# Inverses of triangular blocks in a hybrid recurrent layer: TensorE doubling in place of VectorE steps

## The chip, the core and the metric

One core of a Trainium2 chip runs the whole kernel. The metric is device time in microseconds of one execution. The engines are TensorE (PE, with its weight loads shown as PEld), VectorE (DVE), ScalarE (ACT), GpSimd (POOL) and SyncE (SP, which issues the DMAs). They run beside each other and wait for one another by semaphores.

## What is computed

One layer of a decoder trunk over a prompt of 1024 tokens and 8 sample tokens, width 1024. A normed input is projected to the columns of four mixers (GLA, S5, a gated delta net, RWKV-7), each mixer runs its recurrence, its output is gated, and one output projection and a final norm follow. What matters here are the two mixers with a triangular system per block of 64 tokens. The delta net states it openly:

```python
low = jnp.where(strict, jnp.einsum('nbhid,nbhjd->nbhij', kb, k) * decay, 0.0)
tmat = low + jnp.eye(c, dtype=low.dtype)          # c = 64
sol = lax.linalg.triangular_solve(tmat, rhs, left_side=True, lower=True, unit_diagonal=True)
u, w = sol[..., :HEAD_DIM], sol[..., HEAD_DIM:]
def step(s, inp):                                 # over the blocks of a sequence
    uu, ww, qd, kd, at, gt = inp
    v_new = uu - jnp.einsum('bhcd,bhdv->bhcv', ww, s)
    o = jnp.einsum('bhcd,bhdv->bhcv', qd, s) + jnp.einsum('bhij,bhjv->bhiv', at, v_new)
    s = gt[..., None, None] * s + jnp.einsum('bhcd,bhcv->bhdv', kd, v_new)
    return s, o
```

RWKV-7 is given as a step per token; the kernel brings it to the same blocked form, again with the inverse of a unit lower triangular 64 x 64 matrix per block and head.

## The kernel before

The sequence is worked in two halves of 512 tokens (the second with the 8 sample tokens), and in each half a mixer is two units, one per pair of heads. A unit is a Python generator of stages: its projections, its preparation, for RWKV and the delta net its inverses (stage 2), and the recurrence over eight blocks (stage 3). The string ORDER names the units in the order in which their next stages are emitted (R, D, L for RWKV, delta net and GLA, S for S5, W for S5's weights, g for a gate, a tick for the second half; 97 tokens), and PRI gives a stage a head start in priority ("R2" is stage 2 of an R unit). From that a scheduler that simulates a timeline fixes the order of every engine's queue; on the chip each engine takes its queue strictly in that order.

A projection (`stream`, line 269) loads 128 columns of weights in two quarters by DMA, splits each into two parts (ACT at line 265, POOL at line 266) and runs 24 matmuls per piece of 260 or 512 tokens at line 277. These matmuls are more than half of TensorE's busy time, and the weight loads (line 262) are issued from SP's queue in their turn.

`inverse` (line 287) is called at the start of stage 2 (lines 446 and 656), eight times in all: two mixers, two pairs, two halves. One call inverts 16 matrices of 64 x 64. Each is cut into two 32 x 32 diagonal blocks, so there are 64 blocks, and one block below. Before the change:

- The blocks go from their tiles to DRAM (d1, line 297) and come back in LT with one block per partition, copied to four groups of 32 partitions (line 300); DT is loaded with rows of the unit matrix (dinit).
- 31 steps on VectorE, each a product (line 307, into DP) and a sum (line 309, into DT), build the inverses.
- DT goes to DRAM (d2, line 312) and into the diagonal blocks of XT (line 314).
- Line 318 transposes the first diagonal block on VectorE; the matmuls of lines 323 and 326, eight per parity of the block, each with an eviction by ACT (lines 324 and 327), form the block off the diagonal.

The recurrences (`mm` at lines 483 and 689) then use XT: in each of the eight steps matmuls alternate with VectorE (r, U or UV at line 122, r at line 693, the state at lines 499 and 702) and ACT copies the output (lines 500 and 703). Their PSUM tiles come from `psc`, a tag with four buffers, as do those of `inverse`.

The GLA unit has a loop of six levels whose products `lw0` and `lw1` are put on VectorE or POOL by the table ENG (line 116 executes them).

Of the kernel before, what the change touches and what calls it, by code (L numbers as in the profile page):

```python
# [16 lines left out]
T = 1024  # L17
# [7 lines left out]
NB = dict(ta=9, pr=11, on=3, gp=8, sh=2, kA=6, XT=2, Gt=5, s8=4, ss=4, wr=3, wh=2, wl=2, d1=1, LT=1, DT=2, DP=1, d2=2, Dn=2, w8=2, rf=1,  # L25
# [4 lines left out]
           glu="V", g5="V", cvm="V", l2="V", sgl1="V", sgl2="V", lw0="V", lw1="G", ld0="G", ld1="G", lqk="V", rS="A", rr="V",  # L30
# [18 lines left out]
for _b, _n, _w, _p in (("A", "ident", 128, 128), ("A", "vec", NVEC, 128), ("B", "bones", 128, 128), ("B", "maskG", 256, 128),  # L49
                       ("B", "onesr", 1, 128), ("B", "wlora", 256, 128), ("B", "i64", 64, 128),  # L50
                       ("B", "negD", 128, 128), ("B", "Jm", 128, 128),
                       ("B", "wg2", 256, 16), ("B", "st_shift", 7 * NS, 128), ("B", "st_conv", 18 * NS, 128)):
    CONST[_n] = (_b, CONST_W[_b], _p)
    CONST_W[_b] += _w
# [9 lines left out]
def trunk(ctx: ExitStack, tc: tile.TileContext, I, O):  # L64
# [20 lines left out]
    def cload(name, shape):  # L85
        """A block of columns of the constants that one transfer brings."""
# [7 lines left out]
    def late(ins, after):  # L94
        """Schedule ins, which nothing else holds back, only when after has been issued: its tile waits for its turn."""
# [18 lines left out]
    def tt(name, out, a, b, op=ALU.mult):  # L114
        """out = a op b on the engine that ENG names."""
# [14 lines left out]
    def load_x(h, after=None):  # L130
        """The rows of a half and the gains of its norm."""
# [11 lines left out]
    # ------------------------------------------------------------ constants  # L143
# [10 lines left out]
    i64 = cload("i64", (128, 64))  # L154
    onesr = cload("onesr", (128, 1)).to_broadcast([128, 128])
# [17 lines left out]
    # what is carried from the first half of the sequence to the second  # L173
# [22 lines left out]
    def sig_arg(e, x, bias=None):  # L196
        """e = x (+ bias), bounded where exp(-x) would run out of the range of Ln: 1 / (1 + e^43) < 2^-62."""
# [5 lines left out]
    def sig_chain(e, *outs):  # L203
        """sigmoid(e) to each (out, columns of e)."""
# [8 lines left out]
    def sample_bc(src):  # L213
        """[128 (h, v), 8] -> PSUM [128 (h, any), 8, 64]: each head's values along the free dim."""
# [6 lines left out]
    def mat_vec(S, col):  # L221
        """sum over keys i of S[(h, i), b, v] * col[(h, i), b], on all partitions of the head."""
# [46 lines left out]
    def stream(wsrc, evac):  # L269
        """evac(PSUM [128, m], c0, m) for the columns of (128 columns of w).T @ x."""  # L270
# [15 lines left out]
    # ------------------------------------------------------------ inverses of unit lower triangular matrices  # L286
    def inverse(Ga, XT, after):
        """XT[64 p + s, k, t] = ((I - L) ** -1)[t, s] for the 16 strictly lower L[t, s] = Ga[p][..][s, k, t] of a unit;
        p is the parity of a chunk and k = (pair of chunks, head), in one or two tiles."""
        Q = [(p, f) for p in range(2) for f in range(2)]  # L290
        at = lambda p, f: slice(64 * p + 32 * f, 64 * p + 32 * f + 32)
        d1 = drp.tile([2, 2, 8, 32, 32], F32, tag="d1", bufs=NB["d1"], name="d1")
        for p, f in Q:
            r = slice(32 * f, 32 * f + 32)
            nb = 8 // len(Ga[p])
            for b, g in enumerate(Ga[p]):
                SP.dma_start(out=d1[p, f, nb * b:nb * b + nb].rearrange("(c e) s t -> s c e t", e=2), in_=g[r, :, :, r])
        LT = tmp.tile([128, 32, 32], F32, tag="LT", bufs=NB["LT"], name="LT")
        for q in range(4):
            SP.dma_start(out=LT[32 * q:32 * q + 32], in_=d1.rearrange("p f x s t -> (p f x) s t"))  # L300
        DT = tmp.tile([128, 8, 32], F32, tag="DT", bufs=NB["DT"], name="DT")
        late(SP.dma_start(out=DT.rearrange("p m i -> p (m i)"), in_=I["dinit"]), after)
        for j in range(31):
            m = j // 4 + 1
            w = 31 - j
            tp = tmp.tile([128, 8, 32], F32, tag="DP", bufs=NB["DP"], name="DP")
            V.tensor_tensor(tp[:, :m, :w], DT[:, :m, j:j + 1].to_broadcast([128, m, w]),  # L307
                            LT[:, j:j + 1, j + 1:32].to_broadcast([128, m, w]), ALU.mult)
            V.tensor_tensor(DT[:, :m, j + 1:32], DT[:, :m, j + 1:32], tp[:, :m, :w], ALU.add)  # L309
# [1055 lines left out]
def lay_out(inp):  # L1365
    import numpy as np
    z = lambda *s: np.zeros(s, np.float32)
    a = {}
# [141 lines left out]
```

## Time and profile before

| | us |
|---|---|
| median of 3 runs | 1070.27 |
| lowest, highest | 1069.81, 1078.98 |
| profiled execution, first to last instruction (its span) | 1069.0 |

The profile gives no time of its own for the profiled execution beside its span. The lowest run is 0.8 us above the span, the median 1.3 us: that is what lies around it. Busy time of an engine is the union of its instructions' times; a TensorE record lasts until its results are out, so successive records overlap. The granted clock is the share of 2.4 GHz that TensorE got; 0.5 is the lower of its two levels, and a mean between 0.5 and 1 says how the time was divided.

### The profile page before, as it was taken

The numbers are of one execution on the slowest core, as the hardware profiler recorded it, in microseconds if no ns is written. First come the engines' busy times: TensorE is split into PE (matmuls) and PEld (weight loads), VectorE is DVE, ScalarE is ACT, GpSimd is POOL, SyncE is SP. The second block draws the span as 40 slices with busy tenths as digits, with TensorE's granted clock in tenths as the row PEclk, the third lists the DMA queues.
The fourth block names the chain that finished last, engine by engine and source line by source line (L and its number), as shares of the span: only waits on it lengthen the run. The fifth ranks groups of instructions, "written<-read, shape, count | busy, mean of one in ns | idle before, by whom it ended". The sixth has DMA issues, their size and how long they took to land. (4 is left out here: it accounts for less than half of the span.)

```text
span 1069.0 us, 16993 instructions
## 1 busy us (share of the span) xinstructions
PE 928.3 (87%) x5994; PEld 762.7 (71%) x5994; DVE 704.2 (66%) x1871; ACT 459.6 (43%) x1033; POOL 395.3 (37%) x434
## 2 busy tenths in 40 slices
PE   3899889979999788897989898988989989769794
PEld 3676657658777576797788767677868958658694
DVE  8528884668648864736578989979875366553514
ACT  4355544332644343522753454643235235162634
POOL 2788654531321441133363403125326312313231
PEclk9999979876898666798999889888888569869898
DMA  7133414210211132224223223311112014612532
GB/s 235 50 127 106 115 59 111 71 54 21 74 49 43 46 93 81 81 79 148 69 85 97 77 76 83 92 47 50 53 59 71 22 66 126 212 49 79 183 128 86
DMA packets 76804, 92.23 MB, mean 86 GB/s; under 512 B 41400, under 2 KB 43584, under 8 KB 76720
## 3 DMA queue, kind: packets, MB, share of 16 engines
q1 hardware_dynamic: 76720, 91.16, 27.2%
q8 instruction: 47, 0.77, 0.3%
q14 instruction: 37, 0.30, 0.1%
HBM read 74.38 MB, written 14.62 MB: 83 GB/s over the span
## 5 line engine op out<-in xcount | busy, mean ns | idle before, releaser
L266 POOL TENSOR_TENSOR wl<-wr,wh 128x512 fp32r<-128x512 f32 x152 | 204.6, 1348 | 420.5 <-ACT wh L265 403.6
L277 PE MATMUL psp<-xhi,wh 128*128 128x260 f32 (+2 forms) x728 | 262.2, 361 | 10.7 <-DVE rx L355 6.5
L277 PE MATMUL psp<-xhi,wl 128*128 128x260 f32 (+2 forms) x728 | 256.3, 355 | 5.2 <-POOL wl L266 5.0
L277 PE MATMUL psp<-xlo,wh 128*128 128x260 f32 (+2 forms) x728 | 253.3, 349 | 0.8 <-DVE xlo L257 0.8
L277 PEld LDWEIGHTS psp<-xhi,wh 128*128 128x128 f32 x728 | 153.2, 210 | 33.8 <-issue 12.8
L277 PEld LDWEIGHTS psp<-xhi,wl 128*128 128x128 f32 x728 | 151.2, 209 | 25.4 <-POOL wl L266 7.4
L265 ACT CAST wh<-wr 128x512 fp32r<-128x512 f32 x152 | 93.7, 618 | 172.3 <-PE psp L277 92.9
L277 PEld LDWEIGHTS psp<-xlo,wh 128*128 128x128 f32 x728 | 153.2, 211 | 16.7 <-issue 3.8
L307 DVE TENSOR_TENSOR DP<-DT,LT 128x60 f32<-128x60 f32 (+24 forms) x248 | 81.9, 330 | 12.5 <-DMA XT<-d 3.1
L309 DVE TENSOR_TENSOR DT<-DT,DP 128x60 f32<-128x60 f32 (+24 forms) x248 | 73.8, 297 | 6.1
L277 PE MATMUL psp<-ohi,wh 128*128 128x260 f32 (+1 forms) x192 | 65.5, 342 | 5.4 <-ACT yT L1295 3.5
L277 PE MATMUL psp<-olo,wh 128*128 128x260 f32 (+1 forms) x192 | 64.0, 334 | 1.8 <-DVE olo L116 1.8
L277 PE MATMUL psp<-ohi,wl 128*128 128x260 f32 (+1 forms) x192 | 62.9, 334 | 0.0
L1303 DVE TENSOR_TENSOR xf<-psb,xf 128x128 f32<-128x128 f32 x64 | 14.5, 282 | 49.6 <-PE psb L1301 41.3
L277 PEld LDWEIGHTS psp<-ohi,wh 128*128 128x128 f32 x192 | 37.7, 197 | 8.5 <-ACT yT L1295 3.9
L762 PE MATMUL psb<-W 64*128 64x64 f32 x256 | 40.7, 331 | 1.8 <-DVE DT L309 1.8
L112 ACT ACTIVATE eg<-eg 128x260 f32<-128x260 f32 (+1 forms) x72 | 34.0, 486 | 18.2 <-DVE eg L199 17.4
L277 PEld LDWEIGHTS psp<-olo,wh 128*128 128x128 f32 x192 | 37.7, 196 | 4.6 <-DVE olo L116 2.1
L762 PEld LDWEIGHTS psb<-W 64*128 64x128 f32 x256 | 36.4, 237 | 5.7 <-issue 3.1
L277 PEld LDWEIGHTS psp<-ohi,wl 128*128 128x128 f32 x192 | 37.0, 195 | 2.4 <-POOL wl L266 0.2
L116 POOL TENSOR_TENSOR df<-cum 128x256 f32<-128x256 f32 x48 | 30.8, 663 | 17.2 <-DVE cum L737 15.2
L483 PE MATMUL psc<-UV,Gt 64*128 64x64 f32 (+1 forms) x256 | 35.6, 288 | 0.6 <-ACT UV L476 0.6
(423 smaller groups left out, 1862.4 us busy)
## 6 DMA issues: line engine op xcount, KB each, us to landing
wr<-in_wct SPq DMA_DIRECT2D x120, 256.0 KB
wr<-in_wo SPq DMA_DIRECT2D x32, 256.0 KB
xn<-in_x SPq DMA_DIRECT2D x8, 512.0 KB
LT<-d SPq DMA_DIRECT2D x32, 128.0 KB
xf<-in_x SPq DMA_DIRECT2D x8, 512.0 KB
out_y<-xf SPq DMA_DIRECT2D x8, 512.0 KB
dgp<-gp SPq DMA_DIRECT2D x8, 256.0 KB
Gml<-dG SPq DMA_DIRECT2D x4, 512.0 KB
```

What stands on the lines that cost most here:

```text
L112: A.activation(out, in_, func, bias=bias, scale=scale, **kw)
L116: return (G if ENG[name] == "G" else V).tensor_tensor(out, a, b, op)
L265: A.copy(hi, raw)
L266: G.tensor_tensor(lo, raw, hi, ALU.subtract)
L277: X["mm"] = PE.matmul(p[:, :m], w[:, k % 4, :], x[:, k, c0:c0 + m], start=(k == 0 and s == 0), stop=(k == 7 and s == 2))
L307: V.tensor_tensor(tp[:, :m, :w], DT[:, :m, j:j + 1].to_broadcast([128, m, w]), LT[:, j:j + 1, j + 1:32].to_broadcast([128, m, w]), ALU.mult)
L309: V.tensor_tensor(DT[:, :m, j + 1:32], DT[:, :m, j + 1:32], tp[:, :m, :w], ALU.add)
L483: PE.matmul(o, l, r, start=start, stop=True, skip_group_check=True)
L762: PE.matmul(pg[:, c, :], W[HS[e], t], W[HS[e], t].rearrange("p (b f s) -> p f b s", f=2, s=s)[:, 1], start=True, stop=True)
L1303: V.tensor_tensor(xf[j][:, cols], pt[:, j, :], xf[j][:, cols], ALU.add)
```

## The change

`inverse` builds the 32 x 32 inverses on TensorE by doubling the size of the blocks that are already inverted: 1, 2, 4, 8, 16 to 32. The running inverse is kept in the PSUM tile `acc`. At each of five levels 32 matmuls (four quadrants, eight matrices each) multiply the blocks with the inverse so far (Xn), VectorE evicts the product through a mask that leaves the blocks of this level (LX), 32 more matmuls add the correction to acc, and VectorE transposes acc (Xn) while ACT copies it (Xt) for the next level. The four quadrants lie on the diagonal of the array: rows and columns 32 q to 32 q + 31. The off-diagonal block is formed as before, with both parities in one loop. The DMA round trips, LT, DT, DP and dinit go; two masks of constants, `imask` and `i32`, join the blob constB. The product lw1 goes from POOL to VectorE, five priorities are lowered (R2, D3, L1, R1, L2), and ORDER is rearranged.

```diff
-NB = dict(... d1=1, LT=1, DT=2, DP=1, d2=2, Dn=2, ...
+NB = dict(... LX=2, Xn=2, Xt=2, ...
-ENG = dict(... lw1="G", ...
+ENG = dict(... lw1="V", ...
-PRI = {"R2": 4000, "D2": 1000, "R3": 4000, "D3": 4000, "L1": 2000, "R1": 600, "L0": 100, "L2": 600, "D0": 300, "D1": 1000}
-ORDER = ("x W t W m W R0 g6 R0 D0 W W M W D0 D1 R1 W R0 R1 R0 L0 R1 R1 L0 D1 L0 g0 D0 D0 S g0 L1 g4 g6 g3 g7 L1 D1 g2 D1 g5 "
-         "L1 x' g7 g1 g4 S t' R1' R1' m' R0' g1 R1' g3 M' R1' R0' g2 D0' g5 R0' D1' D0' L1' g1' g7' R0' D0' D1' g4' g6' D0' "
-         "L0' L1' L1' D1' g2' g7' g0' L0' D1' g6' g4' L0' S' g5' g3' S' g3' g0' g2' g5' g1' T T'")
+PRI = {"R2": 620, "D2": 1000, "R3": 4000, "D3": 2000, "L1": 900, "R1": 380, "L0": 100, "L2": 300, "D0": 300, "D1": 1000}
+ORDER = ("x W t W m W g6 R0 D0 R0 W W M W D0 W D1 R1 R1 R0 L0 R1 R1 R0 L0 D1 L0 g0 D0 g0 L1 g4 g6 g3 L1 D1 D0 S g2 g7 D1 g5 L1 "
+         "x' g7 g1 g4 S t' R1' R1' R0' m' g1 R1' g3 R1' R0' D0' L1' M' g2 D0' g5 R0' D1' g1' g7' R0' D0' D1' D0' g4' g6' L0' L1' "
+         "D1' g2' g7' g0' L1' L0' g4' D1' g6' L0' S' g5' g3' g1' S' g3' g0' g2' g5' T T'")
+    imask = cload("imask", (128, 160))
+    i32 = cload("i32", (128, 32))
     def inverse(Ga, XT, after):
         Q = [(p, f) for p in range(2) for f in range(2)]
         at = lambda p, f: slice(64 * p + 32 * f, 64 * p + 32 * f + 32)
...
+        nb = 8 // len(Ga[0])
+        gat = lambda p, f, k, t: Ga[p][k // nb][32 * f:32 * f + 32, k % nb // 2, k % 2, t]
+        one = i32.rearrange("p (o t) -> p o t", o=1).to_broadcast([128, 8, 32])
+        acc = psc(128, 8, 32)
+        def mm(o, l, r, start, first=None):
+            ins = PE.matmul(o, l, r, start=start, stop=True, skip_group_check=True)
+            if first is not None:
+                late(ins, first)
+            return ins
         for p, f in Q:
+            mm(acc[at(p, f)], i32[at(p, f)], one[at(p, f)], True, after)
+        Xn = Xt = one
+        for lv in range(5):
+            pl = psc(128, 8, 32)
+            for k in range(8):
+                for p, f in Q:
+                    mm(pl[at(p, f), k, :], gat(p, f, k, slice(32 * f, 32 * f + 32)), Xn[at(p, f), k, :], True)
+            LX = tmp.tile([128, 8, 32], F32, tag="LX", bufs=NB["LX"], name="LX")
+            V.tensor_tensor(LX, pl, imask[:, 32 * lv:32 * lv + 32].rearrange("p (o t) -> p o t", o=1).to_broadcast([128, 8, 32]), ALU.mult)
+            for k in range(8):
+                for p, f in Q:
+                    mm(acc[at(p, f), k, :], LX[at(p, f), k, :], Xt[at(p, f), k, :], False)
+            Xn = tmp.tile([128, 8, 32], F32, tag="Xn", bufs=NB["Xn"], name="Xn")
+            Xt = tmp.tile([128, 8, 32], F32, tag="Xt", bufs=NB["Xt"], name="Xt")
+            if lv < 4:
+                V.transpose(Xn.rearrange("p k t -> p (k t)"), acc.rearrange("p k t -> p (k t)"))
+                A.copy(Xt, acc)
+        for p, f in Q:
+            A.copy(XT[at(p, f), :, 32 * f:32 * f + 32], acc[at(p, f)])
         for p in range(2):
             late(G.memset(XT[at(p, 1), :, 0:32], 0.0), after)
+            V.transpose(Xn[at(p, 0)], acc[at(p, 0)])
+        po = psc(128, 8, 64)
+        for k in range(8):
+            for p in range(2):
+                mm(po[at(p, 1), k, 0:32], gat(p, 0, k, slice(32, 64)), Xn[at(p, 0), k, :], True)
+        A.copy(Xn[at(0, 1)], po[at(0, 1), :, 0:32])
+        V.tensor_copy(Xn[at(1, 1)], po[at(1, 1), :, 0:32])
+        for k in range(8):
+            for p in range(2):
+                mm(po[at(p, 0), k, 32:64], Xn[at(p, 1), k, :], XT[at(p, 1), k, 32:64], True)
+        A.copy(XT[at(0, 0), :, 32:64], po[at(0, 0), :, 32:64])
+        V.tensor_copy(XT[at(1, 0), :, 32:64], po[at(1, 0), :, 32:64])
```

The lines taken out of `inverse` (293 to 327) are those printed above.

## Rows read from the trace of the kernel before

**Rows 1.** The page, part 1: busy us, share of the span, instructions.
```profile
PE 928.3 (87%) x5994; PEld 762.7 (71%) x5994; DVE 704.2 (66%) x1871; ACT 459.6 (43%) x1033; POOL 395.3 (37%) x434
```

**Rows 2.** Busy time by stage; columns: stage, us, engines, TensorE's clock, DMA, GB/s.
```profile
core 0: us, PE busy (x) PEld busy (x) DVE busy (x) ACT busy (x) POOL busy (x), PEclk, DMA share, GB/s
...
119.00:178.00 59.00, 52.21 (x286) 36.59 (x285) 46.03 (x94) 24.71 (x49) 35.74 (x37) 0.88 0.33 97
178.00:336.00 158.00, 146.01 (x892) 112.48 (x891) 98.13 (x279) 62.77 (x144) 44.37 (x47) 0.81 0.19 54
...
554.00:610.00 56.00, 50.53 (x368) 44.93 (x368) 46.92 (x115) 22.24 (x49) 21.77 (x27) 0.91 0.31 92
610.00:746.00 136.00, 121.74 (x942) 98.90 (x940) 120.53 (x340) 69.35 (x167) 39.46 (x42) 0.87 0.26 71
```

**Rows 3.** Lines 307 and 309: their groups, then VectorE's time in them by stage.
```profile
L307 DVE TENSOR_TENSOR DP<-DT,LT 128x60 f32<-128x60 f32 (+24 forms) x248 | 81.9, 330 | 12.5 <-DMA XT<-d 3.1
L309 DVE TENSOR_TENSOR DT<-DT,DP 128x60 f32<-128x60 f32 (+24 forms) x248 | 73.8, 297 | 6.1
...
119.00:178.00 59.00, 14.34 (x31) 0.88 0.33 97
554.00:610.00 56.00, 10.37 (x31) 0.91 0.31 92
610.00:746.00 136.00, 26.24 (x82) 0.87 0.26 71
...
119.00:178.00 59.00, 10.71 (x31) 0.88 0.33 97
554.00:610.00 56.00, 7.27 (x31) 0.91 0.31 92
610.00:746.00 136.00, 19.82 (x82) 0.87 0.26 71
```

**Rows 4.** Groups by shape: busy us, mean ns of one | idle before, releaser.
```profile
L424 DVE TENSOR_TENSOR bv<-psb,rx 128x260 f32<-128x260 f32 x4 | 1.6, 413 | 0.0
L318 DVE STREAM_TRANSPOSE Dn<-XT 32x256 f32<-32x256 f32 x16 | 6.9, 432 | 6.3 <-DMA XT<-d 6.0
L116 DVE TENSOR_TENSOR W<-l,df 128x256 f32<-128x256 f32 x24 | 13.8, 573 | 2.4 <-ACT df L112 1.8 <-ACT At L766 0.4
L474 ACT COPY Bn<-psc 128x256 f32<-128x256 f32 x16 | 5.9, 371 | 13.8 <-PE psc L473 8.0 <-PE psc L483 5.8
L703 ACT COPY on<-psc 64x128 f32<-64x128 f32 x32 | 8.3, 260 | 42.5 <-DVE state L702 37.0 <-PE psb L1236 5.1
```

**Rows 5.** TensorE's timeline around lines 323, 326 and 759: start, us, instruction, count.
```profile
167.88 0.69 PE L323 MATMUL psc<-Dn,Gt 32*32 32x32 f32 x16
...
172.59 0.40 PE L277 MATMUL psp<-xhi,wh 128*128 128x512 f32 x1
172.83 0.39 PE L277 MATMUL psp<-xlo,wh 128*128 128x512 f32 x1
173.15 0.24 PE L326 MATMUL psc<-XT,Dn 32*32 32x32 f32 x2
...
174.62 0.21 PE L323 MATMUL psc<-Dn,Gt 32*32 32x32 f32 x1
...
174.74 0.57 PE L323 MATMUL psc<-Dn,Gt 32*32 32x32 f32 x13
...
233.50 0.46 PE L759 MATMUL psb<-W 64*32 64x32 f32 x20
...
243.92 1.06 PE L323 MATMUL psc<-Dn,Gt 32*32 32x32 f32 x16
```

**Rows 6.** What TensorE waited for: us in total, times, longest us.
```profile
PE psc L689 <- DVE U L122: 9.2, 7, 2.6
...
PE psc L689 <- DVE state L702: 5.4, 6, 2.1
...
PE psp L277 <- POOL wl L266: 5.0, 5, 2.9
```

More of the change, by code (lines that the diff above doesn't have):

```diff
@@ L29 @@
 ENG = dict(kqo="G", kqi="G", qd="G", kds="V", kd="G", rga="G", rgm="V", rcos="G", k2="V", ari="V", aro="V", bko="G", bki="V",
[L30 removed]
+           glu="V", g5="V", cvm="V", l2="V", sgl1="V", sgl2="V", lw0="V", lw1="V", ld0="G", ld1="G", lqk="V", rS="A", rr="V",
            rU="V", dU="V", fg="V", la="V", tlo="V", cv0="V")
[L32 to L35 removed]
+PRI = {"R2": 620, "D2": 1000, "R3": 4000, "D3": 2000, "L1": 900, "R1": 380, "L0": 100, "L2": 300, "D0": 300, "D1": 1000}
+ORDER = ("x W t W m W g6 R0 D0 R0 W W M W D0 W D1 R1 R1 R0 L0 R1 R1 R0 L0 D1 L0 g0 D0 g0 L1 g4 g6 g3 L1 D1 D0 S g2 g7 D1 g5 L1 "
+         "x' g7 g1 g4 S t' R1' R1' R0' m' g1 R1' g3 R1' R0' D0' L1' M' g2 D0' g5 R0' D1' g1' g7' R0' D0' D1' D0' g4' g6' L0' L1' "
+         "D1' g2' g7' g0' L1' L0' g4' D1' g6' L0' S' g5' g3' g1' S' g3' g0' g2' g5' T T'")
 GORD = ((RWKV, 0), (RWKV, 1), (GDN, 0), (GDN, 1), (GLA, 0), (GLA, 1), (S5, 0), (S5, 1))
@@ L291, in inverse @@
         at = lambda p, f: slice(64 * p + 32 * f, 64 * p + 32 * f + 32)
-        d1 = drp.tile([2, 2, 8, 32, 32], F32, tag="d1", bufs=NB["d1"], name="d1")
-        for p, f in Q:
[L294 to L309, printed above, removed]
@@ L310, in inverse @@
-        d2 = drp.tile([2, 2, 8, 32, 32], F32, tag="d2", bufs=NB["d2"], name="d2")
-        for q in range(4):
-            SP.dma_start(out=d2.rearrange("p f x (m q) i -> q (p f x) m i", q=4)[q], in_=DT[32 * q:32 * q + 32])
+        nb = 8 // len(Ga[0])
[7 more added lines that the diff above has]
+            return ins
@@ L313, in inverse @@
         for p, f in Q:
-            SP.dma_start(out=XT[at(p, f), :, 32 * f:32 * f + 32], in_=d2[p, f].rearrange("x c i -> c x i"))
-        Dn = tmp.tile([128, 8, 32], F32, tag="Dn", bufs=NB["Dn"], name="Dn")
+            A.copy(XT[at(p, f), :, 32 * f:32 * f + 32], acc[at(p, f)])
         for p in range(2):
             late(G.memset(XT[at(p, 1), :, 0:32], 0.0), after)
-            V.transpose(Dn[at(p, 0)], XT[at(p, 0), :, 0:32])
-        pq = psc(128, 8, 32)
-        po = psc(128, 8, 32)
-        for p in range(2):
-            for k in range(8):
-                PE.matmul(pq[at(p, 1), k, :], Ga[p][k // nb][0:32, k % nb // 2, k % 2, 32:64], Dn[at(p, 0), k, :], start=True, stop=True)
-            A.copy(Dn[at(p, 1)], pq[at(p, 1)])
-            for k in range(8):
-                PE.matmul(po[at(p, 0), k, :], Dn[at(p, 1), k, :], XT[at(p, 1), k, 32:64], start=True, stop=True)
-            A.copy(XT[at(p, 0), :, 32:64], po[at(p, 0)])
+            V.transpose(Xn[at(p, 0)], acc[at(p, 0)])
@@ L1449, in lay_out @@
     a["lmask"] = np.concatenate(m, 1).astype(np.float32)
-    di = z(128, 8, 32)
-    for p in range(128):
-        for m in range(8):
-            di[p, m, 4 * m + p // 32] = 1.0
-    a["dinit"] = di.reshape(128, 256)
+    r, c = ii[:, None] % 32, np.arange(32)[None]
+    a["imask"] = np.concatenate([(r // (2 * w) == c // (2 * w)) & (r // w % 2 == 1) & (c // w % 2 == 0) for w in (1, 2, 4, 8, 16)], 1).astype(np.float32)
+    a["i32"] = (r == c).astype(np.float32)
     a["onesr"] = np.ones((128, 1), np.float32)
```

4 lines of the change are left out of this document (2 added, 2 removed).

## The prediction

> **What bounds the kernel now.** I read the page's engine table first, then busy time by stage, then the stage table of the two loops that go, then single instructions, last the waits of TensorE. In the engine table TensorE leads with 928.3 of 1069.0 us, VectorE has 704.2 [rows 1]. By stage, however, the leader changes: from 554 to 746 us, where the second half's RWKV units run, VectorE is busy 46.92 + 120.53 = 167.4 of 192 us (87%), and from 119 to 178 us 46.03 of 59 (78%); from 178 to 336 only 98.13 of 158 (62%) [rows 2]. TensorE's share there (90%) is no throughput: a projection matmul is on record for 0.40 us while the next starts 0.23 to 0.24 us after it [rows 5], so its busy time holds much pipeline that other work could use. Nor has it its full clock: granted are 0.81 to 0.91 in these stages [rows 2], thus between 18 and 38% of the time at 1.2 GHz. So no engine sets the pace of the whole; VectorE does in 554 to 746, and the queue order of TensorE, with waits inside the recurrences, does elsewhere.
>
> The loops that the change removes (lines 307 and 309) hold VectorE for 81.9 + 73.8 = 155.7 us, of which 10.37 + 26.24 + 7.27 + 19.82 = 63.7 us lie between 554 and 746, and 14.34 + 10.71 = 25.1 us in 119 to 178 [rows 3]. That is why the change can pay, and what it must pay with is TensorE time.
>
> **What TensorE gets.** There are eight inverses (two pairs, two halves, two mixers). Before, one has 32 matmuls, each two records (512 records in all, lines 323 and 326, 64 per inverse). After, it has 4 + 5 x 64 + 32 = 356, so 712 records, 704 of them on 32 columns. One quadrant alone starts a record every (0.69 - 0.19) / 15 = 33 ns at full clock, (1.06 - 0.26) / 15 = 53 ns at the low one. Where two quadrants met, 6 records started between 174.62 and 174.74, 20 ns each. Line 759, whose tiles of 64 x 32 lie at several places of the array, gave 20 records in 0.46 us, (0.46 - 0.19) / 19 = 14 ns each [rows 5]. No row has four 32 x 32 quadrants in turn: the price is between 33 / 4 = 8 ns (all four beside each other) and 33 ns (none). I take 14 ns, line 759 being the nearest row. So 704 x 14 = 9.9 us, 0.9 us for the eight wide records (0.4 to 1.7), less 64 x 33 = 2.1: 8.7 us per inverse, 69 us for eight. The four stages average a granted clock of 0.87 [rows 2], so 26% of the time is at the low level, where a record costs 53 instead of 33: times 1.16, 80 us. Each burst also breaks the stream of wide matmuls: 173.15 - 172.83 = 0.32 us where 0.24 is usual, about 0.09 in and as much out [rows 5]. There are 13 bursts instead of 4 per inverse, so 9 x 0.18 x 8 = 13 us. Together TensorE gets +93 us, bounded by 49 (8 ns) and 224 (33 ns).
>
> How much of that shows? At least the 13% in which TensorE is idle covers some, at most all is covered, since records are longer than their pitch. I take half, the middle of the two: +47 us (ends 0 and 0.87 x 224 = 195).
>
> The Trainium skill speaks against this change in one place: TensorEngine Tiling, Gotcha 1 (PSUM Pressure), says that different row tiles cannot use the same PSUM bank at the same time. The four quadrants of a burst are four row tiles and write to one tile of PSUM. The overlapping records at 174.6 us write to two tiles, pq and po, so no run here shows it either way. By that rule the price is that of the serial row, and the sum is the first rival's.
>
> **What VectorE loses and gets.** Per inverse five masked evictions of 128x256 at 413 ns (a PSUM operation on 260 columns), four transposes of 256 columns at 432 ns (the old ones have 32 partitions, as many columns), two copies of at most 413 ns: 4.6 us, 37 us for eight [rows 4]. Line 318's two transposes stay. Edit lw1 moves 24 products from POOL to VectorE, 24 x 0.573 = 13.8 us [rows 4]. Net 155.7 - 37 - 13.8 = 105 us less.
>
> What it is worth by stage: from 554 to 746 lie 31 + 82 = 113 of the second half's 124 steps, 3.65 inverses; 63.7 - 3.65 x 4.6 = 46.9 us go, and with VectorE setting the pace for 87% of the time, -41 us (ends 0 and -47). From 119 to 178: (25.1 - 4.6) x 0.78 = -16 us (0 to -20). The remaining 66.9 us lie where VectorE has room; less 15.4 added that is 51.5, of which I count a quarter, -13 (0 to -32, at 62%). Together -70. lw1 costs +5, a third of its 13.8 (0 to 14), since only some of these products run while VectorE is full.
>
> **Other parts.** ScalarE gets per inverse four copies of acc and, net, two of a quarter of the partitions, at 371 ns each at most: 2.2 us, 18 us for eight [rows 4]; it is busy 22.24 + 69.35 of the 192 us from 554 to 746 [rows 2], 48%, so 0 (ends 0 and 18); without that cover the next level's matmuls wait, for the copy stands beside the transpose of 432 ns and is shorter. The DMA round trip goes: 48 + 32 + 8 + 32 + 32 = 152 issues on SP, behind which weight loads stand. TensorE waited for split weights only 5.0 us in all [rows 6], so at most that is won: -4 (ends 0 and -5). What SP waits for next is POOL's weight split, as before. constB grows by 192 columns; the dinit loads go: 0. PSUM: acc holds one of four psc buffers through the whole inverse, pl one or two more, so recurrence steps beside it have to do with one or two instead of about three; a step's buffer is freed by a copy of 260 ns [rows 4], at worst one such wait in half of 64 steps, 8 us; I take 0, since most steps wait longer elsewhere. Order and priorities: 1069.0 - 928.3 = 141 us of TensorE idle [rows 1] over the 97 tokens of the order is 1.5 us each; 14 of them change place, -21 to +21, and I take 0, as the old trace cannot say which way. The priorities move no work of their own: inside these bounds. The inverse also gets shorter; what runs in the wait is projection work that must be done anyway: 0.
>
> **Sum.** 1069.0 + 47 - 70 + 5 - 4 = 1047 us of span. The runs are 1069.81 to 1078.98, median 1070.27, so some 1 us lies around the span; I keep 1047 (rounding is coarser than this us).
>
> **Rivals.** *Serial quadrants* (slower). If the four quadrants take turns at 33 ns, TensorE gets +224, half shown 112: 1069 + 112 - 70 + 5 - 4 = 1112 us. For it: the only four-row-tile case is untested, and TensorE is the busiest engine. Against it: the two quadrants at 174.6 us kept their own pace side by side. It decides from the point where half of TensorE's extra equals the 69 us won: (138 - 13) / 1.16 / 8 + 2.1 - 0.9 = 14.7 us per inverse, 21 ns per record. Chance 0.22.
>
> *New waits for old ones* (no change). TensorE takes its queue in order; each burst waits for a mask, a transpose or a copy, and behind it stand projections and recurrence steps that could run. In the recurrences, six kinds of wait (three a step, 64 steps, 192 waits) cost TensorE from 9.2 to 5.4 us each, 41.8 in all, 0.22 us per wait [rows 6]. 13 x 8 = 104 bursts at that price are 23 us: 1070. For it: VectorE's queue is long from 554 to 746. Against: it gets shorter. Chance 0.17.
>
> *All in the gaps* (faster still). At 8 ns TensorE gets 49 us; if three quarters vanish in its pipeline gaps, 12 are left: 1069 + 12 - 70 + 5 - 4 = 1012 us. For it: granted clocks of 0.81 to 0.91 show much thin time, and the two-quadrant row. Against: bursts land while projections run too. Chance 0.20. That the change does not do what it says I see no sign of: loops and transfers are gone from the code.
>
> **How the numbers follow.** Forecast 1047, chance 0.41, own range 1030 to 1060. About 1% (10 us) is what a measurement of this kernel can tell from no change. Faster takes the forecast nearly whole (0.38) and the gap case, 0.58; within 1%: three quarters of the waits case and the forecast's upper edge, 0.16; slower: serial quadrants and the rest of the waits, 0.26. For 8 in 10 the range reaches from below the gap case, 1000, to the serial case, 1110.
>
> **What would show it.** VectorE near 600 us; some 5,700 records of 32 x 32 matmuls, started 8 to 20 ns apart inside a burst (33 would show the serial case); no DMA to d; about the same 20 to 30% of low clock; TensorE's waits for LX, Xn and Xt in sum under 25 us (more is the waits case); the second half's RWKV stretch shorter by some 20 us in net. Wrong would be the sum if TensorE's busy time rises with the span by as much as its extra: then nothing was covered.

## The result, and the profile after

The changed kernel takes 1172.8 us (median of 4 runs, 1170.18 to 1176.12), the kernel before 1074.62 us in the same set (1069.81 to 1080.82): a ratio of 1.092 (95% interval 1.086 to 1.099). The forecast was 1047 us with a range up to 1110: wrong in sign, and outside the range.

The page of the kernel after, part 1, as in [rows 1]:

```profile
span 1171.1 us, 26864 instructions
...
PE 1012.5 (86%) x11178; PEld 831.1 (71%) x11178; DVE 612.0 (52%) x1487; ACT 476.1 (41%) x1081; POOL 371.0 (32%) x410
```

VectorE lost 92 us of busy time (704.2 to 612.0), as was meant. TensorE gained 84 us (928.3 to 1012.5) and the span 102. The prediction had named this as the sign that its sum is wrong: TensorE's time rises with the span, so nothing of it was covered.

The groups of the new `inverse` by shape (`mm` in it is now line 302, the mask 316, the transpose 323; columns as in [rows 4]):

```profile
L302 PE MATMUL psc<-Xt,LX 32*32 32x32 f32 x2048 | 30.4, 207 | 9.0 <-DVE LX L316 6.1 <-ACT df L112 1.8 <-issue 1.2
...
L302 PE MATMUL psc<-Xn,Gt 32*32 32x32 f32 x1152 | 20.6, 208 | 10.3 <-DVE Xn L329 5.7 <-DVE Xn L323 4.6
...
L302 PE MATMUL psc<-Xn,Gg 32*32 32x32 f32 x1152 | 19.3, 209 | 7.8 <-DVE Xn L323 3.6 <-DVE nst L1218 2.2 <-DVE Xn L329 2.1
...
L316 DVE TENSOR_TENSOR LX<-psc,constB 128x256 f32<-128x256 f32 x40 | 16.8, 421 | 26.1 <-PE psc L302 25.8
...
L323 DVE STREAM_TRANSPOSE Xn<-psc 128x256 f32<-128x256 f32 x32 | 14.3, 447 | 17.4 <-PE psc L302 17.2
```

2048 records (a matmul is two of them) in 30.4 us of busy time are 15 ns each, about the price of the forecast (14). VectorE's new instructions cost what [rows 4] gave (421 and 447 ns for 413 and 432). The prices of single instructions were right; how they add up to the span was not.

Two bursts on TensorE's timeline (start, us, instruction, count), at full clock (the granted clock from 159.4 to 164.6 us is 1.00):

```profile
159.42 0.75 PE L302 MATMUL psc<-Xn,Gt 32*32 32x32 f32 x64
...
163.77 0.75 PE L302 MATMUL psc<-Xt,LX 32*32 32x32 f32 x64
```

64 records in 0.75 us, the last lasting 0.19: (0.75 - 0.19) / 63 = 9 ns each. The four quadrants do run beside each other, into one tile of PSUM, near the lower bound of 33 / 4.

TensorE's waits inside the inverse (us in total, times, longest):

```profile
PEld psc L302 <- issue: 24.1, 50, 2.3
...
PE psc L302 <- DVE LX L316: 8.3, 10, 2.0
PE psc L302 <- DVE Xn L323: 8.2, 9, 1.8
...
PE psc L302 <- DVE Xn L329: 7.7, 4, 2.9
...
PE psc L302 <- issue: 1.2, 2, 0.8
```

24.2 us for LX and Xn, in 23 waits. The weight loads stood 24.1 us before "issue", that is, for nothing that the profile shows; the matmuls themselves had only 1.2 us of such idle time, in two stops. Where the chain of a level is not covered by other work, it looks like this (TensorE, one inverse of the first half):

```profile
215.50 1.08 PE L302 MATMUL psc<-Xt,LX 32*32 32x32 f32 x64 [1.78 <-ACT df L112]
...
217.33 1.07 PE L302 MATMUL psc<-Xn,Gt 32*32 32x32 f32 x64 [0.76 <-DVE Xn L323]
...
219.04 1.08 PE L302 MATMUL psc<-Xt,LX 32*32 32x32 f32 x64 [0.64 <-DVE LX L316]
...
220.75 1.07 PE L302 MATMUL psc<-Xn,Gt 32*32 32x32 f32 x64 [0.63 <-DVE Xn L323]
```

A burst starts every 1.7 us; 0.63 of them are an idle array, and the burst itself takes 1.07 instead of 0.75, since the clock is at its low level (granted 0.50 from 215 to 222.5 us). A record lasts 0.25 us there, so (1.07 - 0.25) / 63 = 13 ns per record. Where other work stands in between, the level takes longer (all engines, another inverse):

```profile
349.52 0.42 DVE L316 TENSOR_TENSOR LX<-psc,constB 128x256 f32<-128x256 f32 x1
...
350.00 0.57 PE L302 MATMUL psc<-constB,LX 32*32 32x32 f32 x42 [0.22 <-DVE LX L316]
...
352.69 0.38 ACT L324 COPY Xt<-psc 128x256 f32<-128x256 f32 x1 [0.37 <-DVE Xn L323]
...
356.70 0.75 PE L302 MATMUL psc<-Xn,Gg 32*32 32x32 f32 x64
```

The copy to Xt begins at 352.69, when Xn is there, and ends at 353.07, but the next burst starts at 356.70, because projection matmuls stand before it in TensorE's queue.

The stages of the first half's recurrences, columns as in [rows 2]:

```profile
194.00:346.00 152.00, 132.69 (x1442) 103.25 (x1441) 63.22 (x142) 53.97 (x130) 30.38 (x33) 0.67 0.09 24
346.00:500.00 154.00, 128.55 (x1937) 100.00 (x1935) 76.10 (x188) 52.63 (x123) 30.63 (x34) 0.71 0.16 50
```

The granted clock is 0.67 and 0.71 there, against 0.81 in the stage of [rows 2] from 178. Over the whole span of the kernel after:

```profile
core 0: 1171.1 us, clock 0.830
```

Before it was 0.858. So (1 - 0.830) x 2 = 34% of 1171 us, about 398 us, went by at 1.2 GHz, where it was 28%, 304 us.

### The profile page after: what moved, and what is told of

It reads as the page before. It is cut to its first block, busy times and chain, and to the rows that moved or that the text cites. A ratio compares the mean times of both kernels' runs of the same rounds, so it can differ in the third digit from the quotient of the medians.

```text
span 1171.1 us, 26864 instructions
## 1 busy us (share of the span) xinstructions
PE 1012.5 (86%) x11178; PEld 831.1 (71%) x11178; DVE 612.0 (52%) x1487; ACT 476.1 (41%) x1081; POOL 371.0 (32%) x410
## 3 DMA queue, kind: packets, MB, share of 16 engines
q1 hardware_dynamic: 47664, 82.86, 22.9%
## 5 line engine op out<-in xcount | busy, mean ns | idle before, releaser
L279 PE MATMUL psp<-xhi,wh 128*128 128x260 f32 (+2 forms) x728 | 257.0, 354 | 13.4 <-DVE rx L368 6.5
L279 PE MATMUL psp<-xhi,wl 128*128 128x260 f32 (+2 forms) x728 | 250.1, 347 | 6.6 <-POOL wl L268 6.4
L279 PE MATMUL psp<-xlo,wh 128*128 128x260 f32 (+2 forms) x728 | 248.7, 343 | 1.0 <-DVE xlo L259 1.0
L279 PEld LDWEIGHTS psp<-xhi,wh 128*128 128x128 f32 x728 | 149.3, 205 | 33.7 <-issue 11.7
L716 ACT COPY on<-psc 64x128 f32<-64x128 f32 x32 | 8.3, 260 | 86.0 <-DVE state L715 83.9
L116 POOL TENSOR_TENSOR dst<-dst,bv 128x512 f32<-128x512 f32 (+1 forms) x4 | 5.1, 1283 | 119.1 <-ACT dst L112 118.6
L496 PE MATMUL psc<-UV,Gt 64*64 64x64 f32 (+1 forms) x256 | 40.4, 308 | 2.1 <-ACT on L513 1.5
L496 PEld LDWEIGHTS psc<-UV,Gt 64*64 64x64 f32 (+1 forms) x256 | 31.2, 205 | 11.0 <-issue 4.0
L302 PEld LDWEIGHTS psc<-Xt,LX 32*32 32x32 f32 x2048 | 25.3, 119 | 19.1 <-issue 13.2
L302 PE MATMUL psc<-Xt,LX 32*32 32x32 f32 x2048 | 30.4, 207 | 9.0 <-DVE LX L316 6.1
```

Source lines behind the costliest of these rows:

```text
L116: return (G if ENG[name] == "G" else V).tensor_tensor(out, a, b, op)
L279: X["mm"] = PE.matmul(p[:, :m], w[:, k % 4, :], x[:, k, c0:c0 + m], start=(k == 0 and s == 0), stop=(k == 7 and s == 2))
L302: ins = PE.matmul(o, l, r, start=start, stop=True, skip_group_check=True)
L496: PE.matmul(o, l, r, start=start, stop=True, skip_group_check=True)
L716: A.copy(ou[ua, c // 2, :], pc[vk, 0:128])
```

## Experiments

Three readings stood at the start. A: the inverse is not the cause, the new order of units and priorities lost the time. B: TensorE's added records are paid in full, since nothing covers them. D: what costs is the latency of the ten bursts of an inverse, which wait for each other. Where an expectation names a further one, it says what it is. Ratios are to the kernel before on the same chip in the same set (its median was 1070 to 1081 us), with 95% intervals; percents are turned into us on 1075.

**Which part.** *e1*: the changed kernel with the old string, priorities and lw1 on GpSimd.

```diff
-ENG = dict(... lw1="V", ...
+ENG = dict(... lw1="G", ...
-PRI = {"R2": 620, "D2": 1000, "R3": 4000, "D3": 2000, ...
+PRI = {"R2": 4000, "D2": 1000, "R3": 4000, "D3": 4000, ...
-ORDER = ("x W t W m W g6 R0 D0 R0 W W M W D0 W D1 ...
+ORDER = ("x W t W m W R0 g6 R0 D0 W W M W D0 D1 R1 ...
```

> The new inverse with the old ORDER, the old PRI and lw1 back on POOL. Theory A (order and priorities: the new order emits the second RWKV recurrence and the first delta-net preparation so that the chains stand alone): most of the 102 us comes from the order, so this kernel is at 1070 to 1105 us, and the clock in the first half's recurrences is back near 0.8. Theory B (the bursts of small matmuls on TensorE: 5184 more records, 84 us more busy time): this kernel is as slow as the changed one, 1150 to 1190 us. Theory C (VectorE's relief did pay and the bursts cost more than it): 1100 to 1150 us.

Measured 1198.9 us, 1.107 (1.095 to 1.118). A falls: the new inverse loses as much in the old order. *e2*: the reverse, the old inverse with the new string, priorities and lw1.

```diff
-        for lv in range(5):
-            pl = psc(128, 8, 32)
...
+        for j in range(31):
+            m = j // 4 + 1
...
```

> The old inverse (VectorE steps, DMA round trips) with the new ORDER, the new PRI and lw1 on VectorE. Theory A (order): 1130 to 1180 us, near the changed kernel. Theory B (bursts): 1065 to 1085 us, near the kernel before. Theory C: between, 1085 to 1130 us.

Measured 1161.5 us, 1.081 (1.074 to 1.088). So the new order, with lw1 on VectorE, costs the old inverse 87 us by itself, while the new inverse does no worse in it than in the old one (1.092 and 1.107): the two parts don't add up. *e14* splits it: the kernel before with the new priorities alone.

```diff
-PRI = {"R2": 4000, "D2": 1000, "R3": 4000, "D3": 4000, "L1": 2000, "R1": 600, "L0": 100, "L2": 600, ...
+PRI = {"R2": 620, "D2": 1000, "R3": 4000, "D3": 2000, "L1": 900, "R1": 380, "L0": 100, "L2": 300, ...
```

> The kernel before with only the new priorities (R2, D3, L1, R1, L2 lowered); old inverse, old string, lw1 on GpSimd. Nothing is left out. Old inverse with new string, priorities and lw1 took 1161.5 us, 85 more than before. If it is the lowered priority of R2 (the old inverse's steps then stand behind other VectorE work and the recurrences start late): 1120 to 1160. If it is the string: 1070 to 1100.

Measured 1081.5 us, 1.009 (1.004 to 1.014): the priorities cost 10 us; if the parts add up, the string and lw1 together cost the other 77. These two were not separated.

**What the levels cost, and what VectorE's relief is worth.** *e3*: the changed kernel with one of its five levels (four are left out with their evictions, transposes and copies). *e4*: the kernel before with 4 of the 31 VectorE steps (27 are left out).

```diff
-        for lv in range(5):
+        for lv in range(1):
...
-        for j in range(31):
+        for j in range(0, 31, 10):
```

> The changed kernel with one doubling level instead of five (levels 2 to 5 are left out, so the blocks are not inverted): 4096 of 5696 small records, 32 masked evictions, and most of the chain of an inverse go. Theory B (TensorE's time): about 4096 records at 9 to 15 ns, 40 to 60 us less, so 1110 to 1130 us. Theory D (the latency of the inverse, five levels in a row with other work queued between them, holds back the recurrences): 60 to 110 us less, 1060 to 1110 us. Theory A (order): 1135 to 1160 us.

> The kernel before with 4 of the 31 VectorE steps (27 left out, so the blocks are not inverted): 216 products and 216 sums, about 135 us of VectorE, go, the DMA round trips stay. If VectorE sets the pace from 554 to 746 us, as the prediction had it, the time falls by 50 to 75 us, to 995 to 1020 us. If it does not, by 0 to 25 us, to 1045 to 1070 us.

e3 took 1082.5 us, 1.006 (1.002 to 1.011): four levels cost 93 us, 23 each, when everything around them is planned anew. e4 took 1039.4 us, 0.967 (0.957 to 0.977). The page's first line of e4:

```profile
PE 909.2 (88%) x5994; PEld 748.3 (72%) x5994; DVE 590.4 (57%) x1439; ACT 459.4 (44%) x1033; POOL 398.0 (38%) x434
```

VectorE is 114 us less busy (704.2 to 590.4) and the span 36 us shorter: taking the steps out, with nothing put in their place, is worth a third of its busy time. The two runs also give the loss as a path: before to e4 -36, e4 to e3 +42 (new order, lw1, one level, and the last four steps and the DMA round trips gone), e3 to after +93; together +99.

**Records or chain.** *e5*: one of eight matmuls per quadrant in each burst (4480 of 5696 records left out; LX's other columns come from the first). *e6*: the levels don't depend on each other (both operands of the chain replaced by the unit matrix, the transposes read the level's product). *e8*: R2 and D2 at priority 4000, so that bursts go first.

```diff
+                    if k == 0:
                         mm(pl[at(p, f), k, :], gat(...), Xn[at(p, f), k, :], True)
...
-                    mm(acc[at(p, f), k, :], LX[at(p, f), k, :], Xt[at(p, f), k, :], False)
+                    mm(acc[at(p, f), k, :], LX[at(p, f), k, :], one[at(p, f), k, :], False)
...
-PRI = {"R2": 620, "D2": 1000, ...
+PRI = {"R2": 4000, "D2": 4000, ...
```

> The changed kernel with one matmul per quadrant in each of the ten bursts of an inverse instead of eight (seven of eight matrices are left out; the mask is applied to the one product eight times over, transposes and copies stay whole): 4480 of 5696 small records go, the chain of five levels, its waits and the evictions stay. Theory B (TensorE's time for the records and the lower clock with it): 4480 records at 9 to 15 ns, 40 to 67 us less: 1105 to 1132 us. Theory D (the chain's waits in TensorE's queue): less than 25 us, 1148 to 1172 us.

> The changed kernel with all bursts, masks, transposes and copies, but the levels do not feed each other: every burst multiplies with the constant unit matrix, and transposes and copies read the level's own product (what the levels compute is left out). Theory B: unchanged, 1155 to 1180 us. Theory D (five levels in a row, each queued behind projections): 40 us less or more, below 1135 us.

> The changed kernel with stage 2 of R and D units at priority 4000 (620 and 1000 before), so that the scheduler puts an inverse ahead of projections. Theory D: the levels follow each other closer than some 10 us, and the time falls by 20 to 50 us. Theory B: no gain, or a loss, since TensorE then waits in the chain: 1165 to 1200 us.

e5: 1122.9 us, 1.053 (1.047 to 1.059). e6: 1194.3 us, 1.119 (1.112 to 1.126). e8: 1158.3 us, 1.088 (1.078 to 1.099). Without the chain it gets slower, not faster: D falls as the sole cause. But e6 is no clean test. Its bursts, no longer kept apart, run in long rows, and there TensorE stands still for a reason that is explained below; the changed kernel has 1.2 us of it, e6 this:

```profile
PE psc L302 <- issue: 19.3, 12, 3.1
```

That is most of the 21 us by which e6's span is longer (1192.5 and 1171.1). Thinner bursts (e5) give back 42 us, so the records count, but not alone. e8's interval overlaps the changed kernel's: nothing shown.

**TensorE time that nobody waits for.** *e9*: the kernel before, with ten bursts of 32 small matmuls in each inverse whose product is never read (5120 records, nothing taken out). *e12*: the same with four matmuls a burst (640 records).

```diff
+        nb = 8 // len(Ga[0])
+        for lv in range(10):
+            pl = psc(128, 8, 32)
+            for k in range(8):            # e12: range(1)
+                for p, f in Q:
+                    PE.matmul(pl[at(p, f), k, :], Ga[p][...], ident[at(p, f), at(p, f)], start=True, stop=True, ...)
```

> The kernel before (old inverse, old order) with ten extra bursts of 32 matmuls of 32 x 32 per inverse whose results nobody uses: 5120 more records, no new chain, no waits on the other engines but for the bursts' start. Theory B: +60 to +100 us, 1135 to 1180 us, and the granted clock falls below 0.858. Theory D: bursts that nobody waits for sink into gaps, +0 to +30 us, 1070 to 1105 us.

> The kernel before with ten idle bursts of four small matmuls (one per quadrant) in each inverse, for which nobody waits; the run with bursts of 32 had 5120 idle records and took 139 us more. Here there are 80 bursts and 320 matmuls (640 records). Theory of records: 27 ns each as in that run, +17 us: 1080 to 1095 us. Theory of edges (a burst breaks the pipeline of wide matmuls, about 0.2 to 0.4 us each, whatever its length): 80 bursts are +16 to +32 us: 1085 to 1105. Theory of the clock (any small burst lets the granted clock fall): more than +50 us, over 1120.

e9: 1209.2 us, 1.135 (1.129 to 1.141), +145. e12: 1123.0 us, 1.044 (1.033 to 1.055), +47. Idle TensorE work costs more than the whole change. This speaks for B, but 47 us for 640 records fitted no price per record; every variant is also planned anew. *e10* asks if the quadrants' order matters: all eight matmuls of one quadrant, then the next.

```diff
-            for k in range(8):
-                for p, f in Q:
+            for p, f in Q:
+                for k in range(8):
```

> The changed kernel with the two loops of a level in the other order: all eight matmuls of one quadrant, then the next quadrant, so that successive records share their rows and columns of the array. Nothing is left out. In the traces one quadrant alone starts a record every 33 ns at full clock and four in turn every 9 ns. Theory B' (each small record costs TensorE some 20 to 27 ns, mostly in places other than its pitch: instruction supply and the edges of a burst): 5120 records at 33 instead of 9 ns are at most 123 us more at full clock, of which the supply of instructions, which sets the pace already in long bursts, hides up to a half: 1220 to 1300 us. Rival (the four quadrants gain nothing in sum, since the burst is bound by the supply of instructions anyway): 1160 to 1190 us, the changed kernel's own time.

Measured 1291.7 us, 1.201 (1.189 to 1.213), 117 more than the changed kernel. Its burst on the timeline:

```profile
164.31 1.91 PE L302 MATMUL psc<-Xn,Gt 32*32 32x32 f32 x64
```

(1.91 - 0.19) / 63 = 27 ns per record instead of 9: neighbours on one quadrant take turns, neighbours on four don't. 18 ns x 5120 are 92 us at full clock; again all of it, and more, is in the span.

**The same order.** The planner simulates a timeline and shuffles all queues when anything changes. Five runs therefore generate the program twice: first the original, for the order of each engine; then the variant, in which every other instruction is bound to that order (an ordering edge only, no wait).

```diff
+    for order in plan.values():
+        for a, b in zip(order, order[1:]):
+            tc.add_manual_dep(traced[b], names[a], NoSync, reason="plan")
```

*e18* and *e17* are e9 and e12 so held; *e19* is the new inverse in the kernel before, everything outside the inverses held (old string and priorities, lw1 on GpSimd); *e21* and *e22* are e5 and a one-level kernel (the last level kept, four left out), held to the order of the changed kernel.

> The kernel before with ten idle bursts of 32 small matmuls in each inverse (5120 records that nobody waits for), and all its own instructions held to exactly their old order on every engine; only the idle ones are inserted. With a new plan the same records took 139 us. Theory P: the records are paid in full, so 100 to 140 us remain, 1170 to 1215. Rival Q (the planner's new order made up most of it): 15 ns per record and an edge each, 1120 to 1150.

> The kernel before with ten idle bursts of four small matmuls in each inverse (640 records), and all its own instructions held to exactly their old order. With a new plan the same took 45 us. Theory P (records and edges): 640 records at 27 ns are 17 us; 1080 to 1095. Rival Q (it is the planner: any inserted work makes it shuffle the queues, and the new order costs some 30 us by itself): held, the cost is under 17 us, 1072 to 1085. If it stays at 45 us, it is neither, but what a break does to the clock.

> The changed inverse in the kernel before, where every instruction outside the inverses keeps exactly the order of the kernel before on its engine (lw1 on GpSimd, old priorities and string); only the inverses' own instructions are planned. Nothing is left out. Run with the old string and a new plan: 1198.9 us. Theory P (small records cost, whatever the order): 1170 to 1215. Rival Q (the new order of everything else lost the time): 1065 to 1120. In this order the ten bursts of an inverse have little between them, so waits for LX and Xn may add up to 8 x 10 x 1 us to either.

> The changed kernel with one of eight matmuls per quadrant in each burst (4480 records left out, the other seven columns of LX made from the first), and every other instruction held to exactly the order that the changed kernel has on its engine: the planner may not use the room. With a new plan the same cut gave 1122.9 us. Theory P (the records themselves cost: pitch, instruction supply, gaps inside bursts): the same 45 to 55 us go without a new plan, 1115 to 1130. Rival Q (the gain came from the new plan): at most half of it, 1145 to 1165.

> The changed kernel with only the last of its five doubling levels (the other four, 256 matmuls per inverse with their evictions, transposes and copies, are left out), and every instruction outside the inverses held to exactly the order of the changed kernel. With a new plan the same cut gave 1082.5 us. Theory P (levels cost by themselves: records, edges and the waits of the chain, some 22 us each): 1085 to 1110. Rival Q (the planner's new order around them gave back a part): 1120 to 1150.

| run | us | ratio (interval) | planned anew |
|---|---|---|---|
| e18, 5120 idle records | 1196.8 | 1.116 (1.102 to 1.130) | e9 1.135 |
| e17, 640 idle records | 1099.9 | 1.025 (1.011 to 1.039) | e12 1.044 |
| e19, new inverse | 1185.1 | 1.103 (1.090 to 1.116) | e1 1.107 |
| e21, thin bursts | 1142.0 | 1.064 (1.051 to 1.078) | e5 1.053 |
| e22, one level | 1120.0 | 1.044 (1.033 to 1.054) | e3 1.006 |

e19 settles the main question: with every other instruction in its old place the new inverse costs 110 us. The plan is not the cause. Beside the same edit planned anew, the fixed order takes some 20 us off in e17 and in e18 and adds 12 in e21, all with intervals that overlap, and it adds 40 in e22, which is clear of them.

Since e19 and the kernel before have the same order, their projection matmuls can be compared one by one. The lag (start in e19 less start before, worked out from the records' starts) at the last one ahead of each inverse and at the first one behind it:

```text
inverse at (us, e19)  159  249  350  444  617  713  797  915  end
lag ahead, us        -8.6  8.0 22.1 34.8 59.2 59.2 76.8 95.5 114.1
lag behind, us       14.9 21.8 41.2 57.7 60.9 80.1 92.5 112.8
```

It is a staircase. Across the eight inverses the lag grows by 23.5, 13.8, 19.1, 22.9, 1.7, 20.9, 15.7 and 17.3 us, 135 in all; between them it changes by -21 in sum. What was won on VectorE can be seen only in that -21, and perhaps in the 1.7 of one inverse, which lies where VectorE was full before. TensorE's time in the inverse by stretch (line 348 of e19 alone) and its waits there:

```profile
100.00:200.00 100.00, 12.80 (x712) 10.71 (x712) 0.84 0.25 72
200.00:300.00 100.00, 12.72 (x712) 10.67 (x712) 0.74 0.10 33
...
sum 1183.00, PE 101.23 PEld 83.83; mean PE 9.20 PEld 7.62
```
```profile
PE psc L348 <- DVE LX L362: 23.2, 32, 3.0
PE psc L348 <- DVE Xn L369: 18.4, 27, 2.2
PE psc L348 <- DVE Xn L375: 14.5, 7, 2.1
...
PE psc L348 <- issue: 4.4, 7, 1.3
...
PE psc L348 <- DVE Xn L381: 3.2, 3, 1.6
```

An inverse takes TensorE 101.2 / 8 = 12.7 us and the program 135 / 8 = 17. What is between them is waiting: 23.2 + 18.4 + 14.5 + 3.2 = 59.3 us for LX and Xn (lines 375 and 381 are the transposes and an eviction of the last step), and 4.4 at "issue"; the matmuls of the old inverse waited 0.5 us. With the page of e19 the whole loss can be added up:

```profile
PE 1005.2 (85%) x11178; PEld 827.4 (70%) x11178; DVE 616.0 (52%) x1463; ACT 477.5 (40%) x1081; POOL 395.8 (33%) x434
```

TensorE is busy 77 us longer than before (1005.2 less 928.3), it stands 63 us longer before the inverse's matmuls, and 26 us less elsewhere (its idle time is 178.2 us of 1183.4, where it was 140.7 of 1069.0): 114 in all, the difference of the spans. So in a fixed order the chain of D stands beside the records of B with nearly as much, though it is not the sole cause. The lower clock did not lengthen the other matmuls: those outside the inverses are busy 909.8 us in e19 and 908.0 before.

**Where the price of an idle record comes from.** e18 less e17 is 97 us for 4480 records, 22 ns each, though four quadrants in turn need 9 to 13. A long run of them in e18, and the page's line for the instruction queue before and in e18:

```profile
360.81 2.90 PE L306 MATMUL psc<-constA,Gg 32*32 32x32 f32 x222
365.14 2.13 PE L306 MATMUL psc<-constA,Gg 32*32 32x32 f32 x128 [1.43 <-issue]
368.59 2.60 PE L306 MATMUL psc<-constA,Gg 32*32 32x32 f32 x128 [1.32 <-issue]
372.04 2.60 PE L306 MATMUL psc<-constA,Gg 32*32 32x32 f32 x128 [0.85 <-issue]
375.77 0.74 PE L306 MATMUL psc<-constA,Gg 32*32 32x32 f32 x34 [1.13 <-issue]
```
```profile
q8 instruction: 87, 1.43, 0.5%
```
```profile
q8 instruction: 47, 0.77, 0.3%
```

(The first of the two is e18, 87 packets of 1.43 MB, the second the kernel before.) TensorE stops after every 128 records, with nothing to wait for in the profile. Two of the periods are 3.45 us long, 27 ns per record, whether the 128 themselves take 2.13 or 2.60. A packet is 1.43 MB / 87 = 16 KB. In the stretch from 360 to 377 (the first line is the share of the DMA engines in 40 slices of it) five packets move, and nothing else:

```profile
DMA  0000001000000010000000100000001000000001
...
DMA packets 5, 0.08 MB, mean 5 GB/s; under 512 B 0, under 2 KB 0, under 8 KB 0
...
q8 instruction: 5, 0.08, 1.9%
```

Four pauses, and four of the packets in step with them: TensorE has run out of instructions. The whole run bears this out. e18 has 40 packets more than the kernel before for 5120 records more, 128 records each. It has 28 such stops (27 before small matmuls); counted through all of TensorE's instructions (a record is two, a weight load and a matmul), every one lies at the same place of a block of 256, to within one, and each ends 2.3 to 2.7 us after a packet of this queue starts. The stops and TensorE's busy time in e18:

```profile
PE psc L306 <- issue: 47.2, 27, 3.4
```
```profile
PE 1006.4 (84%) x11114; PEld 833.1 (70%) x11114; DVE 703.8 (59%) x1871; ACT 459.3 (38%) x1033; POOL 395.3 (33%) x434
```

Of the 124 us that e18 costs, 78 are busy time of TensorE (1006.4 less 928.3) and 47 are these stops; the rest of its idle time is as before (139 and 141 us), so the PSUM buffers that the idle bursts take cost nothing that shows. Over the whole run the gaps between starts of neighbouring small records add up to 77 us where they are under 100 ns (17 before) and to 63 us where they are longer (1 before), 53 of them at the stops: half of the price is the pitch, and most of the other half is supply. The Trainium skill (Runtime: NRT & Kernel Launch, Instruction fetch mechanics) says that instructions come in blocks of 16 KiB, 256 of them, which agrees with 128 records and as many weight loads, and that this is hidden behind the rate of issue, which does not agree with these pauses of 0.85 to 1.43 us.

The changed kernel's bursts are only 64 long and mostly stand alone, and it has only two such stops, 1.2 us. There a record costs less: e21 less after is 30 us for 4480 records, 7 ns each. The rest of its price hangs on the burst and the level (e22, four levels at the same order: 52 us, of which four fifths of e21's 30, 24, are records). The waits for LX and Xn fall from 24.2 us to 5.9 in e22, so up to 18 of the other 28 are waits of the chain. How the rest divides between broken pipeline and lower clock is left open.

**A better version?** *e11*: the first level on VectorE, four on TensorE, R2 and D2 at 4000. *e15*: the kernel before with the new inverse only for RWKV's second half, where VectorE was full (LX and Xn have one buffer each instead of two). Both were planned anew.

```diff
-        for lv in range(5):
+        V.tensor_tensor(Xt[...], src, imask[..., 160:192]..., ALU.mult); V.tensor_tensor(Xt, Xt, one, ALU.add); V.transpose(Xn, Xt)
+        for lv in range(1, 5):
...
-        inverse(...)
+        (inverse_te if h else inverse)(...)      # RWKV only
```

> The changed kernel with the first of its five levels made on VectorE (a masked copy of the blocks plus the unit matrix, and one transpose) and stages R2 and D2 at priority 4000. Nothing is left out. The kernel with one level of five took 1082.5 us, so one level costs about 22 us, and the priorities alone gave 14. If levels add up (theory B): 1172.8 - 22 - 14 = 1137, plus some 5 for the three VectorE instructions, 1130 to 1150 us. If the cost is a threshold of the clock and not a sum over levels, one level less changes nothing: 1155 to 1170 us.

> The kernel before, with its own order, priorities and lw1, that uses the new inverse only for RWKV in the second half (two of eight inverses), where VectorE was busy 87% of the time; there is one buffer instead of two for one transposed tile. Nothing is left out. If the price is 110 us for 5632 small records wherever they lie, two inverses cost 27 us and save VectorE 40 us in the stretch that it bounds; at the payoff that the run with 4 of 31 steps showed, a third, that is 13: +10 to +18 us, 1080 to 1090. If VectorE's bound counts in full in that stretch as the prediction had it (41 us for 3.65 inverses, 22 for two), less half of the TensorE cost: 1060 to 1070.

e11: 1144.7 us, 1.064 (1.053 to 1.076): a level less, with the priorities, takes 30 us off, about what it would if levels add up; the plan changed with it. e15: 1102.0 us, 1.025 (1.016 to 1.033): even two inverses of eight, at the place that favours them, lose 26 us, some of which may be the plan. No run of a whole computation beats the kernel before.

## Why the prediction was wrong

*TensorE +93, half covered, +47.* This step failed. The raw sum was fair: 14 ns per record was to be 9 (full clock) to 13 (low), and TensorE's busy time rose by 84. "I take half" had no row behind it, and the argument for it, that a projection matmul is on record for 0.40 us while the next starts after 0.24, was a wrong reading: in e18 TensorE's busy time rises by 78 us for records that nobody waits for, and all of it is in the span, so there was no such room. Even with nothing covered the sum fell short: 5120 idle records in the same order cost 124 us (e18), where 14 ns each are 72, since 47 us of pauses for instructions come on top.

*Waits of the chain, 0.* The sum has no term for them; they stand only in a rival. They are 24.2 us in the changed kernel and 59.3 in e19.

*Switching, 0.18 us a burst, +13.* Perhaps too small. e17 has 80 bursts of eight records: 27 us (12 to 42), 0.34 us a burst (0.15 to 0.53), the records included; 0.18 is not excluded.

*VectorE -105 of busy time, worth -70.* Mis-sized by two. e4, planned anew, measures 36 us for 114 (25 to 46 by its interval); in e19 the lag falls by 21 between the inverses. The forecast let VectorE set the pace of 554 to 746 for 87% of the time; only one inverse there came out near zero (+1.7), the next cost 20.9.

*Order and priorities 0, bounds 21.* The bounds were wrong: e2 shows +87 with the old inverse (lw1 is in it, for which the forecast had 14 at most). They were worked out from TensorE's idle time per token, as if a token's place could cost only its own idle time. With the new inverse the order does no harm that can be told apart (e1 and the changed kernel: 1.107 and 1.092).

*DMA -4, psc 0, ScalarE 0.* No run tests these by themselves, and none speaks against them. The packets did go, 76,804 to 47,786.

*The clock.* The share of low clock was taken as unchanged at 20 to 30%; it went from 28 to 34%. The 0.87 for the four stages weighs them alike; by their length it is 0.85, which would have made 80 us 81.

Put together by the path through e4 and e3: -36 instead of -70, +42 for order, lw1 and the first level instead of +5 and a fifth of 47, +93 for four levels instead of four fifths of 47. In a fixed order four levels cost 52 (e22), so 41 us of this path are the planner's. By e19, where the other instructions keep their order, it is +77 of TensorE's time instead of +47, +63 of waiting before its new matmuls instead of 0, and -26 elsewhere instead of -70.

*Rivals.* Serial quadrants, the only slower one, named the right sign and 1112 us, by the wrong mechanism: a record takes 9 ns in a burst, not 33. The rule of the Trainium skill behind it (TensorEngine Tiling, Gotcha 1: PSUM Pressure, that different row tiles cannot use one PSUM bank at once) does not hold for these four quadrants, which write to partitions of their own: 64 records into one tile took 0.75 us, and e10 shows what turns would cost. New waits for old ones gave 23 us, and 24.2 were measured. That is luck: 23 waits of 1.05 us, not 104 of 0.22, and 59.3 us in a fixed order. All in the gaps fell with the same step as the forecast.

## What to carry to other kernels

Before moving work to an engine that leads the table, put the same amount of idle work on it, with every other instruction held in its order: two runs (e4 without the old work, e18 with the new load) give -36 and +124. The sign is right, and the size only by some luck, since e18 has 47 us of stops for instructions that the changed kernel lacks, and lacks the waits of its chain; an idle load says nothing of waits. Records that overlap were no sign of room here: cover has to be shown by a run, not by a share. And where a planner orders the queues, its shuffle can weigh as much as the edit (40 us between e3 and e22), so compare variants in a fixed order.

## What the hardware showed that was not expected

- Four 32 x 32 quadrants on the diagonal of the array share one tile of PSUM at 9 ns a record at full clock; the same records ordered by quadrant take 27 (e10).
- Small matmuls can outrun their own instructions: in the long runs of e18 TensorE stops at every 128th record, 28 times for 0.35 to 3.4 us, one 16 KB packet each, and from one stop to the next it takes 3.45 us or more, 27 ns per record. e10, whose records start 27 ns apart in a burst, has no such stop.
- In such a run the clock was low, too: from 360.8 to 376.4 us in e18 TensorE issues nothing but small matmuls, and the granted clock of the stretch is 0.67 (columns as in [rows 2]), so two thirds of it at 1.2 GHz:

```profile
360.80:376.40 15.60, 10.25 (x642) 8.60 (x640) 1.83 (x7) 0.00 (x0) 0.00 (x0) 0.67 0.02 4
```
